# A written order for the last z units and the first gate pair of an encoder layer

## The chip, the core and the metric

The kernel runs on one core of a Trainium2 chip. A core has engines that run side by side, each with its own queue, taken in order: TensorE (PE; its weight loads are shown apart as PEld) multiplies matrices into banks of PSUM, VectorE (DVE) and ScalarE (ACT) work on elements, GpSimd (POOL) does a little of the rest, and SyncE (SP) issues transfers between the chip's memory and the on-chip buffers. The metric is device time in microseconds; lower is better. A run is repeated, and the median of the runs is the kernel's time. The profile comes from one execution of its own.

## The reference, cut to what matters

One layer: `h = RMSNorm(x)` with 16 meta tokens in front (1040 rows of 1024), one input projection `h @ w_in`, and its columns split into q, k, v, z, beta, a, three inputs of a short convolution, and two merge gates A and B of 1024 columns each. Then

```python
y_a = o_dn @ w_branch_dn[l]                      # gated DeltaNet over q, k, v, with silu(z)
y_b = (sc_b * depthwise_conv_centred(sc_c * sc_x, sc_conv_w[l])) @ w_branch_sc[l]
merged = jax.nn.sigmoid(gate_a) * y_a + jax.nn.sigmoid(gate_b) * y_b
h_res = h_res + merged @ w_out[l]
```

and a SwiGLU block and a last norm behind it. All is float32. The change concerns columns of `z`, of `gate_a` and of `gate_b`, and the start of `y_b`.

## The kernel before, in words

**Numbers in two parts.** Each float32 operand of a large product is split into a high and a low part (`split`, L100: ScalarE casts the high part, VectorE subtracts it from the source to get the low part). A product is three matmuls: high x high, high x low, low x high. So a weight of 128 columns (a *unit*, loaded by `wload`, L117) needs one transfer into a raw buffer, one cast on ScalarE (`wh`) and one subtraction on VectorE (`wl`) before its third matmul can run. `dense` (L129) runs the 8 x 3 matmuls of one unit with 512 rows of the activations.

**Phase 1** (to L1395) computes q, k and v, the DeltaNet scans, the short convolution, five of the eight z units (`ZH = 5`) and the gates of the first four column groups (`GH = 4`). It is written out by hand for every engine (`tc.manual_schedule()`, L1035). When its buffers are closed, the pool `tp` takes their place (L1399).

**The z section** (L1475 to L1487) computes the z units 5, 6 and 7. For each unit and each half of the rows: 24 matmuls into a bank (`psany` deals out the eight banks in turn), a tanh on ScalarE (L1485) and a finish on VectorE (L1486) that reads the bank; then a store to `z_d`. The weights have two buffers for `wh` and two for `wl`, so a third unit waits until the first one's matmuls are done. There are four raw buffers.

**The sums of blocks.** The gates 4 to 7 come in pairs, gate A and gate B of the same group, by a Strassen-like scheme with seven products of 512 x 512 blocks instead of eight. It needs sums of blocks of the activations, T1 to T4, which `moving_sums` (L1442) forms once: three or so VectorE operations of 128x2048 for each (`sub`, L179; `add`, L1409), then a split of each into a tile of its own (b0 to b3). Its work tiles are mA (t1, t2) and mB (t3 and a spare, d_). T2 is made from T1's sum, T4 from T2's.

**The pairs.** `pair` (L1492) loads the two weights rg and ru, splits rg whole (A11, A12) and the lower half of ru (A22), forms four sums of the weights' blocks in place (`sums`, L1414) and splits them into a tile `s_hl` (`stationary2`, L1421), which lies in mB for the pairs 0 and 2, in mA for 1 and 3. Then the products (`product`, L1434, 12 matmuls each, L1440) in the order A11 x B11, A12 x B21, S2 x T2, S1 x T1, S3 x T3, S4 x B22, A22 x T4; several of them add to a bank that ScalarE or VectorE has read in between. The last pair has an order of its own: S2, S3, S1, A22 x T4, A11, A12, S4.

**The branch.** Behind the pairs the short convolution's output p is loaded (L1570): its groups 0 to 3 into `mg[0]`, which lies in mA, 4 and 5 into two of four 128x1024 buffers (`s4`), 6 and 7 into raw buffers. It is split into b0 to b3, where T1 to T4 were (high parts in b0 and b1, low parts in b2 and b3). The first unit of `w_branch_sc` is multiplied with all eight groups, one after the other. The merge then writes `mg[0]` and `mg[1]` (mA and mB).

**Who sets the order.** Outside the hand-written stretches a planner orders each engine's queue when the program is built: by priority, earlier lines first, and by the times at which it reckons operands to be ready. Each queue then runs in that order, whatever the chip's times are. `tc.manual_schedule(engines=...)` holds the operations that are issued inside it, on the engines named, to the order in which they are written. Before the change the z section and the pairs are all left to the planner.

Of the kernel before, what the change touches and what calls it, by code (L numbers as in the profile page):

```python
# [8 lines left out]
F32 = mybir.dt.float32  # L9
# [7 lines left out]
P = 128  # L17
D = 1024
KT = 8
SEQ = 1024  # L20
META = 16
L = SEQ + META
C0 = 48
LP = C0 + L
H = 8
# [3 lines left out]
ZH = 5  # L29
GH = 4  # L30
# [7 lines left out]
def unit(col):  # L38

    return (col if col < OBA else col - 32) // P  # L40
# [8 lines left out]
def encoder_layer(ctx: ExitStack, tc: tile.TileContext, x, meta, norm1_w, w_in, w_ba,  # L49
# [3 lines left out]
    x, out = x[0], out[0]  # L53
# [15 lines left out]
    def s4(n=1024):  # L69
        return tp.tile([P, 1024], F32, tag="s4", name=uid("s4"), bufs=4)[:, :n]  # L70
# [29 lines left out]
    def split(hi, lo, src):  # L100
        nc.scalar.copy(hi, src)  # L101
        nc.vector.tensor_tensor(out=lo, in0=src, in1=hi.bitcast(F32), op=ALU.subtract)  # L102
# [14 lines left out]
    def wload(src, j):  # L117
        wh, wl, raw = staged([P, KT, P])
        nc.sync.dma_start(raw, src[j])
        split(wh, wl, raw)  # L120
        return wh, wl
# [7 lines left out]
    def dense(po, w, xx, t0, n, m=P):  # L129
        wh, wl = w  # L130
        xh, xl = xx
        for k in range(KT):
            xhk, xlk = (x[k] if isinstance(x, list) else x[:, k] for x in (xh, xl))
            mm(po[:m, :n], wh[:, k, :m], xhk[:, t0:t0 + n], start=(k == 0), stop=False)  # L134
            mm(po[:m, :n], wh[:, k, :m], xlk[:, t0:t0 + n], start=False, stop=False)  # L135
            mm(po[:m, :n], wl[:, k, :m], xhk[:, t0:t0 + n], start=False, stop=(k == KT - 1))  # L136
# [41 lines left out]
    def sub(out, a, b):  # L178
        nc.vector.tensor_tensor(out=out, in0=a, in1=b, op=ALU.subtract)  # L179
# [1221 lines left out]
    def big(tag, shape, dtype=F32R):  # L1401
        return tp.tile(shape, dtype, tag=tag, name=uid(tag))
# [9 lines left out]
    mov = {}  # L1412

    def sums(rg, ru, s2, s4_, s3, s1):  # L1414
        g0, g1, u0, u1 = rg[:, 0:4], rg[:, 4:8], ru[:, 0:4], ru[:, 4:8]
        nc.vector.tensor_tensor(out=s1, in0=u0, in1=u1, op=ALU.add)
        sub(s3, g0, u0)
        sub(s2, s1, g0)
        sub(s4_, g1, s2)

    def stationary2(j, ru, sa, sb, A_):  # L1421

        for i, r in enumerate((sa, sb)):
            sh, sl = (s_hl[j % 2][:, m, i] for m in range(2))
            split(sh, sl, r)
            for x, n in enumerate((("S2", "S4"), ("S3", "S1"))[i]):
                A_[n] = sh[:, 4 * x:4 * x + 4], sl[:, 4 * x:4 * x + 4]

# [13 lines left out]
    def moving_sums():  # L1442

        c = [slice(C0 + META + 512 * i, C0 + META + 512 * i + 512) for i in range(2)]
        f = lambda m: m.bitcast(F32)
        h0, h1 = ([f(hx[0][:, 4 * i:4 * i + 4, cc]) for cc in c] for i in range(2))
        l0, l1, l2 = ([f(t[:, :, cc]) for cc in c] for t in low_tiles)
        for i in range(2):
            for j in range(2):
                mov[f"B{i + 1}{j + 1}"] = hx[0][:, 4 * i:4 * i + 4, c[j]], [hx[1][4 * i + k][:, c[j]] for k in range(4)]  # L1450
        for i, n in enumerate(("T1", "T2", "T3", "T4")):
            t = big(f"b{i}", [P, 2, 4, 512])
            mov[n] = t[:, 0], t[:, 1]
        x, y = (big(g, [P, 2, 4, 512], F32) for g in ("mA", "mB"))
        t1, t2, t3, d_ = x[:, 0], x[:, 1], y[:, 0], y[:, 1]
        a, b = slice(0, 2), slice(2, 4)
        sub(t1, h0[1], h0[0])
        sub(d_, l0[1], l0[0])
        add(t1, t1, d_)
        split(*mov["T1"], t1)  # L1460
        sub(t2, h1[1], t1)
        add(t2[:, a], t2[:, a], l1[1])
        add(t2[:, b], t2[:, b], l2[1])
        split(*mov["T2"], t2)
        sub(t3, h1[1], h0[1])
        sub(d_[:, a], l1[1], l0[1][:, a])
        sub(d_[:, b], l2[1], l0[1][:, b])
        add(t3, t3, d_)
        split(*mov["T3"], t3)
        sub(t1, h1[0], t2)  # L1470
        add(t1[:, a], t1[:, a], l1[0])
        add(t1[:, b], t1[:, b], l2[0])
        split(*mov["T4"], t1)

    raw_slots.extend((tp, f"raw{i}") for i in range(2))  # L1475
    weights_z = [wload(w_in, unit(OZ + ZH * P))]
    moving_sums()
    for h in range(ZH, H):
        w = weights_z.pop() if weights_z else wload(w_in, unit(OZ + h * P))
        sz = s4(SEQ)  # L1480
        for i in range(2):
            po = psany()
            dense(po, w, hx, C0 + META + 512 * i, 512)
            sl = slice(512 * i, 512 * i + 512)
            nc.scalar.activation(sz[:, sl], po, AF.Tanh, scale=0.5)  # L1485
            nc.vector.scalar_tensor_tensor(out=sz[:, sl], in0=sz[:, sl], scalar=1.0, in1=po, op0=ALU.add, op1=ALU.mult)  # L1486
        nc.sync.dma_start(z_d[h], sz)  # L1487

    left, right = slice(0, 512), slice(512, 1024)
    half_turn = lambda o: nc.scalar.activation(o, o, AF.Tanh, scale=0.5)  # L1490

    def pair(n, j):  # L1492

        last = j == KT - 1
        s_hl[n % 2] = big(("mB", "mA")[n % 2], [P, 2, 2, KT, P])
        if n == 0:
            u = big("w2", [P, 2, 4, P])
            u_hl[0] = u[:, 0], u[:, 1]
        elif n == 1:
            u_hl[1] = [tp.tile([P, 4, P], F32R, tag="t2", name=uid("u_hl"), bufs=2) for _ in range(2)]  # L1500
        gh, gl = wtiles([P, KT, P])
        rg, ru = (rawtile([P, KT, P]) for _ in range(2))
        nc.sync.dma_start(rg, w_in[unit(OGA + j * P)])
        nc.sync.dma_start(ru, w_in[unit(OGB + j * P)])
        A_ = {"A11": (gh[:, 0:4], gl[:, 0:4]), "A12": (gh[:, 4:8], gl[:, 4:8])}
        o1, o2 = s4(), s4()
        bank = pss()
        if not last:
            split(gh, gl, rg)
            product(bank, A_["A11"], "B11")  # L1510
            nc.scalar.copy(o1[:, left], bank)
            po = psz()
            product(po, A_["A12"], "B21")
            add(o1[:, left], po, o1[:, left])
            half_turn(o1[:, left])
        split(*u_hl[n % 2], ru[:, 4:8])
        A_["A22"] = u_hl[n % 2]
        if last:
            split(gh, gl, rg)
        sums(rg, ru, rg[:, 0:4], rg[:, 4:8], ru[:, 0:4], ru[:, 4:8])  # L1520
        stationary2(n, ru, rg, ru, A_)
        bank2 = psz()
        if not last:
            product(bank, A_["S2"], "T2", True)
            nc.scalar.copy(o1[:, right], bank)
            product(bank2, A_["S1"], "T1")
            nc.scalar.copy(o2[:, right], bank2)
            product(bank, A_["S3"], "T3", True)
            add(o2[:, right], bank, o2[:, right])
            half_turn(o2[:, right])  # L1530
            product(bank2, A_["S4"], "B22", True)
            add(o1[:, right], bank2, o1[:, right])
            half_turn(o1[:, right])
            product(bank, A_["A22"], "T4", True)
            nc.scalar.activation(o2[:, left], bank, AF.Tanh, scale=0.5)
        else:
            product(bank, A_["S2"], "T2")
            nc.scalar.copy(o1[:, right], bank)
            product(bank, A_["S3"], "T3", True)
            nc.scalar.copy(o2[:, right], bank)  # L1540
            product(bank2, A_["S1"], "T1")
            add(o2[:, right], bank2, o2[:, right])
            product(bank, A_["A22"], "T4", True)
            po = psz()
            product(po, A_["A11"], "B11")
            nc.scalar.copy(o1[:, left], po)
            add(o2[:, left], bank, o1[:, left])
            half_turn(o2[:, left])
            add(o2[:, right], o2[:, right], o1[:, left])
            half_turn(o2[:, right])  # L1550
            add(o1[:, right], o1[:, right], o1[:, left])
            product(po, A_["A12"], "B21", True)
            nc.scalar.activation(o1[:, left], po, AF.Tanh, scale=0.5)
            product(bank2, A_["S4"], "B22", True)
            add(o1[:, right], bank2, o1[:, right])
            half_turn(o1[:, right])
        nc.sync.dma_start(ta_d[j], o1)
        nc.sync.dma_start(tb_d[j], o2)
        return o1

    for n, j in enumerate(range(GH, KT)):
        o1 = pair(n, j)

    warm2 = keep.tile([P, 1], F32, name="warm2")
    nc.scalar.activation(warm2, o1[:, SEQ - 1:SEQ], AF.Silu)
    mg = [big("mA", [P, 4, SEQ], F32), big("mB", [P, 4, SEQ], F32)]
    px = four("p")
    for j in range(KT):
        pr = mg[0][:, j] if j < 4 else s4(SEQ) if j < 6 else rawtile([P, SEQ])
        nc.sync.dma_start(pr, p_d[j])  # L1570
        split(px[0][j], px[1][j], pr)
    ox = (ap_.tile([P, KT, SEQ], F32R, tag="ah", name="oh"), eighths(low([SEQ])))
# [130 lines left out]
    t = KT - 1  # L1703
# [229 lines left out]
```

## Time and profile before

| what | us |
|---|---|
| median of 3 runs (2020.31 to 2021.19) | 2020.97 |
| the profiled execution | 2023.88 |
| its span, first to last instruction | 2022.2 |
| TensorE busy in the span | 1980.3 |
| VectorE busy | 1398.3 |
| ScalarE busy | 838.1 |
| mean granted clock of TensorE | 0.992 |

Times in the views count from the span's start; the z section begins at about 971 and the branch at about 1095. In a row of a timeline stand the start, the length, engine, line of the program, operation, the tile written and the tiles read, and the count of merged instructions; in brackets, the idle time before it and what ended it. A line is often that of a helper: L102 is the subtraction of any split, L101 its cast, L179 any `sub`, L1409 any `add`, and L134 to L136 the three matmuls of `dense`. Tiles are named without their numbers: `b` is any of b0 to b3, `s` any of the `s4` buffers, `pd`, `pe` and `pm` are banks. Matmuls overlap, so the length of one (0.39 us for 512 columns) is more than the step from one to the next.

### The profile page before, as it was taken

What the parts mean: (1) busy time and instruction counts of PE and PEld (TensorE: products, weight loads), DVE (VectorE), ACT (ScalarE), POOL (GpSimd) and SP (SyncE); (2) the same over time, 40 slices, a digit from 0 to 9 for tenths busy, and PEclk for the clock granted to TensorE, in tenths of its full rate; (3) what the DMA queues carried; (4) which work ended last, traced back from release to release, by engine and by line L of the source; (5) the groups of instructions that cost most, each with busy time, mean ns of one, the idle gap of its engine ahead of it and who ended that gap; (6) DMA issues with size and microseconds to landing.
All of it is one profiled execution on the core that took longest, in us unless ns stands there. A gap on an engine that the chain in (4) does not pass through costs nothing.

```text
span 2022.2 us, 31878 instructions
## 1 busy us (share of the span) xinstructions
PE 1980.3 (98%) x12011; PEld 1724.5 (85%) x12011; DVE 1398.3 (69%) x3013; ACT 838.1 (41%) x1961; POOL 109.2 (5%) x407
## 2 busy tenths in 40 slices
PE   9999999999999999999798999999999999999998
PEld 8998889899999999999687888887878888888887
DVE  6887678877888888855854544468856567656575
ACT  6463464536463646333244221224323333334344
POOL 2011101010201010100000000000000000000000
PEclk9999999999999999999899999999999999999999
DMA  3123231222221212121236643123665345477654
GB/s 136 62 88 100 74 94 59 95 58 85 64 69 59 74 58 74 58 74 53 83 115 243 223 147 116 58 89 106 237 219 209 136 165 175 159 270 245 195 175 166
DMA packets 131121, 251.00 MB, mean 124 GB/s; under 512 B 45013, under 2 KB 54662, under 8 KB 128535
## 3 DMA queue, kind: packets, MB, share of 16 engines
q1 hardware_dynamic: 130391, 247.92, 36.7%
q8 instruction: 94, 1.54, 0.3%
q10 hardware_dynamic: 576, 1.05, 0.1%
q14 instruction: 60, 0.49, 0.1%
HBM read 180.67 MB, written 68.25 MB: 123 GB/s over the span
## 4 chain that ended last, share of the span: by engine, by line
PE 88%; DVE 6%; DMA 3%; ACT 2%; issue 1%; SPq 0%; DVEq 0%; ACTq 0%
PE pm L341 32%; PE pd L1440 11%; PE pe L1440 5%; PE pm L1440 3%; PE pd L903 1%; PE pd L882 1%; PE pd L866 1%; PE pe L603 1%; PE pd L136 1%; PE pd L135 1%; PE pd L134 1%; PE pd L869 1%; PE pe L1839 1%; PE pe L1841 1%; PE pe L1840 1%; PE pd L899 1%
## 5 line engine op out<-in xcount | busy, mean ns | idle before, releaser
L341 PE MATMUL pm<-hTh,wh 128*128 128x512 f32 (+4 forms) x1296 | 446.9, 350 | 0.4 <-ACT hTh L1103 0.2
L341 PE MATMUL pm<-al,wh 128*128 128x512 f32 (+4 forms) x1296 | 446.2, 349 | 0.0
L341 PE MATMUL pm<-hTh,wl 128*128 128x512 f32 (+4 forms) x1296 | 444.1, 348 | 0.0
L341 PEld LDWEIGHTS pm<-hTh,wh 128*128 128x128 f32 x1296 | 242.9, 189 | 13.6 <-issue 0.8
L341 PEld LDWEIGHTS pm<-al,wh 128*128 128x128 f32 x1296 | 243.1, 189 | 12.4 <-issue 0.4
L341 PEld LDWEIGHTS pm<-hTh,wl 128*128 128x128 f32 x1296 | 243.1, 189 | 12.3 <-issue 0.4
L102 DVE TENSOR_TENSOR al<-raw,ring_h 128x1024 fp32r<-128x1024 f32 x73 | 88.8, 1223 | 65.3 <-ACT ring_h L101 64.5
L101 ACT CAST ring_h<-raw 128x1024 fp32r<-128x1024 f32 x73 | 76.6, 1053 | 108.5 <-PE pd L1841 33.7
L990 DVE TENSOR_TENSOR wl<-raw,wh 128x512 fp32r<-128x512 f32 x118 | 79.5, 688 | 30.6 <-ACT wh L993 30.2
L363 DVE SCALAR_TENSOR_TENSOR kq<-ra,wc,kq 128x520 f32<-128x520 f32 x128 | 96.8, 756 | 4.9 <-ACT kq L393 3.6
L889 ACT ACTIVATE w<-pd,small 128x128 f32<-128x128 f32 x128 | 40.0, 364 | 117.0 <-PE pd L882 116.5
L101 ACT CAST wh<-raw 128x1024 fp32r<-128x1024 f32 x47 | 49.4, 1051 | 91.5 <-PE pe L135 27.4
L496 DVE TENSOR_TENSOR tm<-fP,fN 128x135 f32<-128x135 f32 (+23 forms) x248 | 72.2, 291 | 4.9 <-DVE fP L500 0.2
L500 DVE TENSOR_TENSOR fP<-fP,tm 128x135 f32<-128x135 f32 (+23 forms) x248 | 71.7, 289 | 5.1
L993 ACT CAST wh<-raw 128x512 fp32r<-128x512 f32 x118 | 69.2, 621 | 3.7 <-issue 3.6
L102 DVE TENSOR_TENSOR wl<-raw,wh 128x1024 fp32r<-128x1024 f32 x47 | 57.4, 1220 | 8.1 <-ACT wh L101 8.0
L1409 DVE TENSOR_TENSOR b<-pd,b 128x512 f32<-128x512 f32 x22 | 15.2, 690 | 68.5 <-PE pd L1440 68.5
L1776 ACT ACTIVATE b<-b 128x512 f32<-128x512 f32 x22 | 13.9, 632 | 116.4 <-DVE b L1409 116.4
L856 ACT ACTIVATE jk<-NP 128x128 f32<-128x128 f32 x64 | 19.9, 310 | 83.6 <-DVE NP L852 82.6
L876 DVE SCALAR_TENSOR_TENSOR r<-pd,negEG,vS 128x128 f32<-128x128 f32 x120 | 36.8, 345 | 25.5 <-PE pd L866 24.9
L1440 PE MATMUL pd<-b_hl,wh 128*128 128x512 f32 x176 | 54.4, 390 | 0.0
L912 DVE SCALAR_TENSOR_TENSOR S<-S,eGl,pd 128x128 f32<-128x128 f32 x104 | 31.6, 342 | 30.4 <-PE pd L899 30.0
(588 smaller groups left out, 4696.1 us busy)
## 6 DMA issues: line engine op xcount, KB each, us to landing
raw<-in_w_in_dram SPq DMA_DIRECT2D x72, 512.0 KB
raw<-in_w_gate_up_dram SPq DMA_DIRECT2D x44, 512.0 KB
sums<-in_w_down_dram SPq DMA_DIRECT2D x22, 512.0 KB
t_d<-sums SPq DMA_DIRECT2D x11, 1024.0 KB
raw<-s_d SPq DMA_DIRECT2D x44, 256.0 KB
raw<-t_d SPq DMA_DIRECT2D x44, 256.0 KB
act_d<-b SPq DMA_DIRECT2D x43, 256.0 KB
raw<-act_d SPq DMA_DIRECT2D x33, 256.0 KB
```

What stands on the lines that cost most here:

```text
L101: nc.scalar.copy(hi, src)
L102: nc.vector.tensor_tensor(out=lo, in0=src, in1=hi.bitcast(F32), op=ALU.subtract)
L341: mm(po[:, :n], ww[:, k], f(k)[:, t0:t0 + n], start=i == 0, stop=i == 3 * KT - 1)
L363: nc.vector.scalar_tensor_tensor(out=acc, in0=raw[:, h0 + t:h0 + t + hn], scalar=wc[:, t, col:col + 1], in1=acc, op0=ALU.mult, op1=ALU.add)
L496: nc.vector.tensor_tensor(out=tv, in0=fP[:, 0:r, j:j + 1].broadcast_to([P, r, n]), in1=fN[:, j:j + 1, j + 1:32].broadcast_to([P, r, n]), o ...
L500: nc.vector.tensor_tensor(out=fP[:, 0:r, j + 1:32], in0=fP[:, 0:r, j + 1:32], in1=tv, op=ALU.subtract)
L876: nc.vector.scalar_tensor_tensor(out=r0[d], in0=b1[:, d], scalar=negEG[:, c, hd[d]:hd[d] + 1], in1=vS[:, c], op0=ALU.mult, op1=ALU.add)
L889: nc.scalar.activation(w[d], b2[:, 2 + d], AF.Copy, scale=ce[:, c, d:d + 1])
L912: nc.vector.scalar_tensor_tensor(out=Sn, in0=S[d], scalar=eGl[:, cd[d], hd[d]:hd[d] + 1], in1=b1[:, d], op0=ALU.mult, op1=ALU.add)
L990: nc.vector.tensor_tensor(out=u[1][1][:, k], in0=u[2][:, k], in1=u[1][0][:, k].bitcast(F32), op=ALU.subtract)
L993: nc.scalar.copy(u[1][0][:, k], u[2][:, k])
L1440: mm(po, x[:, k], y, start=k + i == 0 and not add_to, stop=k == 3 and i == 2, skip_group_check=add_to)
```

## The change

Three things are changed.

1. The z section and pair 0 stand inside a written order for VectorE and TensorE (`border0`), closed behind pair 0. ScalarE and SyncE are still ordered by the planner. Inside, the sums of blocks are cut into four steps (`moving_sums` becomes a generator), and so are the three z units (`z_rows`), with a step's end behind each tanh; the steps are dealt out by hand: T1, weights of unit 6, left half of unit 5, right half, T2, weights of unit 7, the last finish of unit 5, the loads of pair 0, left half of unit 6, first split of pair 0, right half of unit 6, the other splits and the sums of pair 0's weights, left half of unit 7, T3, right half of unit 7, T4, last finish, pair 0. A finish stands at the start of the step behind its tanh's.
2. `pair` is divided into `pair_weights` (buffers, loads, and two functions that issue the splits and sums) and the products. For the pairs 1 to 3 the order of issue stays as it was. The work tile of T3 and the spare move from mB to b3, and T4's tile is taken from b3 behind them; mB is first taken by pair 0's `s_hl`.
3. The groups 0 to 3 of p are loaded into `mg[1]` (mB) instead of `mg[0]` (mA), since `GH % 2 == 0` is 1. Where the merge writes stays as it was.

The diff:

```diff
@@ -1448,50 +1448,58 @@
         for i in range(2):
             for j in range(2):
                 mov[f"B{i + 1}{j + 1}"] = hx[0][:, 4 * i:4 * i + 4, c[j]], [hx[1][4 * i + k][:, c[j]] for k in range(4)]
-        for i, n in enumerate(("T1", "T2", "T3", "T4")):
+        for i, n in enumerate(("T1", "T2", "T3")):
             t = big(f"b{i}", [P, 2, 4, 512])
             mov[n] = t[:, 0], t[:, 1]
-        x, y = (big(g, [P, 2, 4, 512], F32) for g in ("mA", "mB"))
+        x, y = (big(g, [P, 2, 4, 512], F32) for g in ("mA", "b3"))
         t1, t2, t3, d_ = x[:, 0], x[:, 1], y[:, 0], y[:, 1]
         a, b = slice(0, 2), slice(2, 4)
         sub(t1, h0[1], h0[0])
         sub(d_, l0[1], l0[0])
         add(t1, t1, d_)
         split(*mov["T1"], t1)
+        yield
         sub(t2, h1[1], t1)
         add(t2[:, a], t2[:, a], l1[1])
         add(t2[:, b], t2[:, b], l2[1])
         split(*mov["T2"], t2)
+        yield
         sub(t3, h1[1], h0[1])
         sub(d_[:, a], l1[1], l0[1][:, a])
         sub(d_[:, b], l2[1], l0[1][:, b])
         add(t3, t3, d_)
         split(*mov["T3"], t3)
+        yield
+        t = big("b3", [P, 2, 4, 512])
+        mov["T4"] = t[:, 0], t[:, 1]
         sub(t1, h1[0], t2)
         add(t1[:, a], t1[:, a], l1[0])
         add(t1[:, b], t1[:, b], l2[0])
         split(*mov["T4"], t1)
+        yield
 
     raw_slots.extend((tp, f"raw{i}") for i in range(2))
-    weights_z = [wload(w_in, unit(OZ + ZH * P))]
-    moving_sums()
-    for h in range(ZH, H):
-        w = weights_z.pop() if weights_z else wload(w_in, unit(OZ + h * P))
+    left, right = slice(0, 512), slice(512, 1024)
+    border0 = ExitStack()
+    border0.enter_context(tc.manual_schedule(engines={mybir.EngineType.DVE, mybir.EngineType.PE}))
+    z_units = [wload(w_in, unit(OZ + ZH * P))]
+
+    def z_rows(h):
+
         sz = s4(SEQ)
-        for i in range(2):
+        for sl in (left, right):
             po = psany()
-            dense(po, w, hx, C0 + META + 512 * i, 512)
-            sl = slice(512 * i, 512 * i + 512)
+            dense(po, z_units[h - ZH], hx, C0 + META + sl.start, 512)
             nc.scalar.activation(sz[:, sl], po, AF.Tanh, scale=0.5)
+            yield
             nc.vector.scalar_tensor_tensor(out=sz[:, sl], in0=sz[:, sl], scalar=1.0, in1=po, op0=ALU.add, op1=ALU.mult)
         nc.sync.dma_start(z_d[h], sz)
-
-    left, right = slice(0, 512), slice(512, 1024)
+        yield
+
     half_turn = lambda o: nc.scalar.activation(o, o, AF.Tanh, scale=0.5)
 
-    def pair(n, j):
-
-        last = j == KT - 1
+    def pair_weights(n, j):
+
         s_hl[n % 2] = big(("mB", "mA")[n % 2], [P, 2, 2, KT, P])
         if n == 0:
             u = big("w2", [P, 2, 4, P])
@@ -1503,22 +1511,35 @@
         nc.sync.dma_start(rg, w_in[unit(OGA + j * P)])
         nc.sync.dma_start(ru, w_in[unit(OGB + j * P)])
         A_ = {"A11": (gh[:, 0:4], gl[:, 0:4]), "A12": (gh[:, 4:8], gl[:, 4:8])}
+
+        def first():
+            split(gh, gl, rg)
+
+        def second():
+            split(*u_hl[n % 2], ru[:, 4:8])
+            A_["A22"] = u_hl[n % 2]
+            sums(rg, ru, rg[:, 0:4], rg[:, 4:8], ru[:, 0:4], ru[:, 4:8])
+            stationary2(n, ru, rg, ru, A_)
+        return A_, first, second
+
+    def pair(n, j, A_, first, second):
+
+        last = j == KT - 1
         o1, o2 = s4(), s4()
         bank = pss()
         if not last:
-            split(gh, gl, rg)
+            if n:
+                first()
             product(bank, A_["A11"], "B11")
             nc.scalar.copy(o1[:, left], bank)
             po = psz()
             product(po, A_["A12"], "B21")
             add(o1[:, left], po, o1[:, left])
             half_turn(o1[:, left])
-        split(*u_hl[n % 2], ru[:, 4:8])
-        A_["A22"] = u_hl[n % 2]
         if last:
-            split(gh, gl, rg)
-        sums(rg, ru, rg[:, 0:4], rg[:, 4:8], ru[:, 0:4], ru[:, 4:8])
-        stationary2(n, ru, rg, ru, A_)
+            first()
+        if n:
+            second()
         bank2 = psz()
         if not last:
             product(bank, A_["S2"], "T2", True)
@@ -1558,15 +1579,37 @@
         nc.sync.dma_start(tb_d[j], o2)
         return o1
 
+    sums_of_blocks = moving_sums()
+    z0, z1, z2 = (z_rows(h) for h in range(ZH, H))
+    next(sums_of_blocks)
+    z_units.append(wload(w_in, unit(OZ + (ZH + 1) * P)))
+    next(z0)
+    next(z0)
+    next(sums_of_blocks)
+    z_units.append(wload(w_in, unit(OZ + (H - 1) * P)))
+    next(z0)
+    pair0 = pair_weights(0, GH)
+    next(z1)
+    pair0[1]()
+    next(z1)
+    pair0[2]()
+    next(z1)
+    next(z2)
+    next(sums_of_blocks)
+    next(z2)
+    next(sums_of_blocks)
+    next(z2)
     for n, j in enumerate(range(GH, KT)):
-        o1 = pair(n, j)
+        o1 = pair(n, j, *(pair_weights(n, j) if n else pair0))
+        if n == 0:
+            border0.close()
 
     warm2 = keep.tile([P, 1], F32, name="warm2")
     nc.scalar.activation(warm2, o1[:, SEQ - 1:SEQ], AF.Silu)
     mg = [big("mA", [P, 4, SEQ], F32), big("mB", [P, 4, SEQ], F32)]
     px = four("p")
     for j in range(KT):
-        pr = mg[0][:, j] if j < 4 else s4(SEQ) if j < 6 else rawtile([P, SEQ])
+        pr = mg[GH % 2 == 0][:, j] if j < 4 else s4(SEQ) if j < 6 else rawtile([P, SEQ])
         nc.sync.dma_start(pr, p_d[j])
         split(px[0][j], px[1][j], pr)
     ox = (ap_.tile([P, KT, SEQ], F32R, tag="ah", name="oh"), eighths(low([SEQ])))
```

## The prediction

> **What bounds the kernel now.** I read the page first, then the list of waits of TensorE, then the stretches around the two long waits, then the chain and the timelines of the engines there.
>
> ```profile
> PE 1980.3 (98%) x12011; PEld 1724.5 (85%) x12011; DVE 1398.3 (69%) x3013; ACT 838.1 (41%) x1961; POOL 109.2 (5%) x407
> PE pd L136 <- DVE wl L102: 11.5, 1, 11.5
> PE pd L134 <- ACT b L101: 6.0, 1, 6.0
> 992.90:1006.40 13.50, 1.97 (x8) 0.99 (x6) 13.50 (x11) 5.07 (x4) 0.00 (x0) 0.70 0.12 47
> 1006.40:1012.20 5.80, 5.79 (x14) 4.59 (x15) 5.73 (x6) 0.99 (x2) 0.00 (x0) 0.52 0.49 163
> 1094.70:1100.70 6.00, 0.01 (x1) 0.00 (x0) 3.34 (x4) 4.09 (x5) 0.00 (x0) 0.72 0.99 358
> 1100.70:1104.20 3.50, 3.44 (x7) 2.32 (x8) 2.10 (x2) 1.50 (x2) 0.00 (x0) 0.51 1.01 410
> ```
>
> TensorE is busy 98% of the span, so only its waits can be won. The two longest stand at the two ends of the stretch that the change touches; the columns of a stretch are length, busy time of PE, PEld, DVE, ACT and POOL, then the granted clock. Each wait is followed by a stretch at half clock: 5.8 us at 0.52 and 3.5 us at 0.51, a further loss of 5.8 x 0.48 = 2.8 us and 3.5 x 0.49 = 1.7 us.
>
> Why the first wait? The timeline of VectorE (first column the start, second the length):
>
> ```profile
> 961.04 1.23 DVE L102 TENSOR_TENSOR wl<-raw,wh 128x1024 fp32r<-128x1024 f32 x1
> 962.18 1.53 DVE L416 SCALAR_TENSOR_TENSOR rb<-ra,cols,rb 128x512 f32<-128x512 f32 x2
> 971.05 0.69 DVE L451 TENSOR_TENSOR rb<-pm,rb 128x512 f32<-128x512 f32 x1 [4.70 <-PE pm L341]
> 971.91 1.23 DVE L102 TENSOR_TENSOR wl<-raw,wh 128x1024 fp32r<-128x1024 f32 x1 [0.17 <-ACT wh L101]
> 973.91 2.29 DVE L179 TENSOR_TENSOR mA<-hTh 128x2048 f32<-128x2048 f32 x1 [0.77 <-DMA p_d<-rb]
> 976.12 2.28 DVE L179 TENSOR_TENSOR mB<-al 128x2048 f32<-128x2048 f32 x1
> 980.52 2.29 DVE L1409 TENSOR_TENSOR mA<-mA,mB 128x2048 f32<-128x2048 f32 x1
> 982.72 0.68 DVE L1486 SCALAR_TENSOR_TENSOR s<-s,pm 128x512 f32<-128x512 f32 x1
> 987.72 2.35 DVE L1409 TENSOR_TENSOR mA<-mA,al 128x1024 f32<-128x1024 f32 x2
> 1005.14 1.22 DVE L102 TENSOR_TENSOR wl<-raw,wh 128x1024 fp32r<-128x1024 f32 x1
> 1010.33 0.69 DVE L1416 TENSOR_TENSOR raw<-raw 128x512 f32<-128x512 f32 x1
> 1011.66 0.68 DVE L102 TENSOR_TENSOR u_hl<-raw,u_hl 128x512 fp32r<-128x512 f32 x1
> ```
>
> The low parts of units 5 and 6 were cut at 961.04 and 971.91, that of unit 7 only at 1005.14, behind 31 us of sums for T1 to T4. TensorE had nothing else that was ready. The section's account, from TensorE's rows:
>
> ```profile
> 1026.52 2.72 PE pe L1440 x12
> 1034.51 2.88 PE L1440 MATMUL pd<-b,w 128*128 128x512 f32 x12
> 1053.55 2.88 PE L1440 MATMUL pd<-b,u_hl 128*128 128x512 f32 x12
> ```
>
> Twelve matmuls take 2.72 us, 0.227 each. From 971.05 (phase 1's last product is done there, its reader L451 starts) three z units of 48 are 32.6 us and two gate pairs of 84 are 38.1, together 70.7. The other two rows are the last products, A22 x T4, of pairs 0 and 1. Pair 1 so ends at 1053.55 + 2.72 = 1056.3, so 85.2 us were spent: **14.5 us** are the wait and its slow clock.
>
> **The change, part by part.**
>
> *1. The first half of the section.* No operation goes and none comes; the order changes. A full-width sum starts 2.2 us after the one before it (973.91, 976.12), two half-width ones are 2.27, a cut of one weight 1.14 to the next start, a z finish (L1486) 0.60, each of the four 512-wide sums 0.69. Written order adds what the planner had avoided: behind each T-block's sums stands its cut, which waits for ScalarE's cast:
>
> ```profile
> 983.19 1.90 ACT L101 CAST b<-mA 128x2048 fp32r<-128x2048 f32 x1
> 1011.83 1.05 ACT L101 CAST mB<-raw 128x1024 fp32r<-128x1024 f32 x1 [1.05 <-DVE raw L179]
> ```
>
> With 0.1 us on either side that is a hole of 2.1 us on VectorE for each T-block and 1.15 for a weight. The sums cannot start before 973.91, because the first is released by the last store of phase 1 and that does not move. Then:
>
> - T1: 3 x 2.2 + 2.1 + 2.2 = 10.9, to 984.8; unit 6's low part to 986.0. Before, it was done at 973.1. TensorE needs it at 971.05 + 10.88 + 0.45 = 982.4, so there is a **new wait of 3.7 us**, queued behind T1 on VectorE. Should unit 5's cut now also stand behind phase 1's last operation (971.74), 1.4 us of the 3.7 fall at unit 5; the sum is the same.
> - T2: 2.2 + 2.27 + 2.1 + 2.2 = 8.8; with two z finishes and unit 7's low part, VectorE is at 997.0 and unit 7's part is ready at 996.5. TensorE ends unit 6 at 986.05 + 46 x 0.227 = 996.5: **no wait for unit 7**, the 11.5 us are gone.
> - Pair 0's first cut needs unit 6's buffers, free at 996.5, and a cast: 998.9. Finish, 22-block, four sums, a hole of 1.15, two cuts, finish: 1006.9. TensorE comes to pair 0 at 1007.4, so its weights cost nothing; unit 7's matmuls cover them.
> - T3 is 11.0, to 1017.9; a finish and T4 8.8, to 1027.2; then a finish and two of pair 0's additions, the second of which must have read the bank that A22 x T4 adds to: **1029.1**.
>
> TensorE, from 1007.4, runs A11, A12, S2, S1 to 1018.3 (T3 is in time), S3 and S4 to 1023.7. Then the last product would wait 5.4 us for T4: that is late next.
>
> Whether TensorE stands still there depends on the planner. It holds only operations inside the written order to that order, and before's trace shows it slipping others in: the cut at 961.04 belongs to unit 5, but stands between two operations of phase 1, which is in written order. The second such border, behind the merge, shows the same:
>
> ```profile
> 1397.01 0.69 DVE L102 TENSOR_TENSOR u_hl<-raw,u_hl 128x512 fp32r<-128x512 f32 x1
> 1400.41 0.68 DVE L1416 TENSOR_TENSOR raw<-raw 128x512 f32<-128x512 f32 x1
> 1401.86 2.29 DVE L102 TENSOR_TENSOR b<-al,b 128x2048 fp32r<-128x2048 f32 x1
> 1403.01 0.73 PE L1440 MATMUL pe<-s,s_hl 128*128 128x512 f32 x2 [0.62 <-ACT s_hl L101]
> 1404.20 4.38 PE L1440 MATMUL pd<-b,w 128*128 128x512 f32 x11 [0.47 <-DVE b L102]
> ```
>
> There the weight sums of the next pair (1397.01, 1400.41) stand ahead of the written T4 cut at 1401.86, and a piece of the next pair's product ran while A22 x T4 waited. TensorE was not in written order there, so for it this is an inference from VectorE. I take it that pair 1's A11 and A12, 5.4 us, fill the gap. Pair 1's cuts and sums (1.1 + 0.6 + 2.8 = 4.5 us) then slip into VectorE's holes for T3 and T4 (2 x 2.1); what doesn't fit delays the written chain, between 0.3 us and all 4.5, and I take 1.5, since the holes are nearly as long as the work. That makes about 0.6 us of wait at S3, 0.8 at A22 and 0.5 at pair 1's S2.
>
> Sum: 3.7 + 0.6 + 0.8 + 0.5 = 5.6 us of waits instead of 14.5: **8.9 us won** by the end of pair 1. The pairs behind it leave VectorE room to catch up (third and fourth number: 19 us of TensorE, 8.95 of VectorE):
>
> ```profile
> 1037.30:1056.30 19.00, 19.00 (x86) 15.73 (x85) 8.95 (x11) 7.69 (x12) 0.00 (x0) 1.00 0.31 111
> 962.30 0.34 SPq L1504 DMA_DIRECT2D raw<-in_w_in_dram  x1
> ```
>
> The queue of SyncE: pair 0's second load left at 962.30 already (second row), into the raw buffer that unit 5 gives up, and the written order doesn't hold SyncE. The three z stores leave with the right-hand finishes, near 997, 1007 and 1028 by the sums above; pair 1 needs the last of their buffers for o2 only after its S1 product, some 12 us later. I cost them at nothing.
>
> *2. The branch operands.*
>
> ```profile
> 1072.75 5.44 PE pd L1440 x24
> 1083.76 2.72 PE pd L1440 x12
> 1086.48 8.24 PE pe L1440 x36
> 1094.74 4.86 DMA mA<-p_d
> 1099.62 1.05 ACT b L101
> 1083.86 0.69 DVE L1409 TENSOR_TENSOR s<-pe,s 128x512 f32<-128x512 f32 x1 [10.37 <-PE pe L1440]
> 1086.58 1.23 DVE L102 TENSOR_TENSOR b<-s,b 128x1024 fp32r<-128x1024 f32 x1 [2.03 <-PE pd L1440]
> 1093.79 1.23 DVE L102 TENSOR_TENSOR wl<-raw,wh 128x1024 fp32r<-128x1024 f32 x1 [0.78 <-ACT wh L101]
> ```
>
> mA holds the last pair's weights, read until 1094.7; only then does the load start, and load, cast and semaphores are the 6.0 us. mB holds pair 2's, whose last reader ends at 1072.75. The four loads (4 of 512 KB, 5.8 us at the 358 GB/s of the stretch above) can be in by about 1082. Their cuts go where T1 and T3 lay, free at 1083.76. What is late next is those cuts: four casts, 4 us, and four subtractions, 4.6 us, beside the last three products, 8.2 us. VectorE stood idle 10.4 us before 1083.86 and 2.03 + 0.78 = 2.8 us from there to 1094.7, so some of the later additions move past the end, but the branch's first matmuls need only the first operands, one each 0.45 us or more. I cost this at nothing; if the cover were short, it would be up to 2 us. **Won: 6.0 + 1.7 = 7.7 us.**
>
> Moving T3's work tile from mB to b3 costs nothing by itself: T4 takes b3 after T3's cut in the same order.
>
> Together 16.6 us. The profiled execution took 2023.88 us with a span of 2022.2, 2.9 above the median of 2020.97; differences carry over, so **2020.97 - 16.6 = 2004.4**.
>
> *A rule weighed.* After the broken-up waits at 1401.8 the clock fell as well:
>
> ```profile
> 1404.20:1408.60 4.40, 4.39 (x12) 3.50 (x13) 2.89 (x4) 0.85 (x2) 0.00 (x0) 0.61 0.75 253
> ```
>
> That was 2.60 + 0.62 + 0.47 = 3.7 us of waiting, 4.4 x 0.39 = 1.7 us lost. The Trainium skill (TensorE: Matmul & The Clock Gate, Part 1: The HAM clock gate) says the clock halves after an idle window of about 3.4 us, whose phase is free, and comes back after as much work. By that rule the new 3.7 us wait just reaches the point, and would cost an estimated 1.7 us; the trace agrees with it at 3.7, 6.0 and 11.5 us.
>
> **The rivals.**
>
> - *Nothing fills the T4 gap* (TensorE's written order lets nothing by). Against it: the rows of 961.04 and 1397.01; for it: TensorE itself isn't shown. Waits 3.7 + 5.4, and 1.7 of slow clock as after the 6.0 us wait: 10.8, won 3.7 + 7.7 = 11.4, **2009.6**.
> - *The clock falls at unit 6.* For it: the row at 1404.20; against it: unit 5's share may cut the wait in two. 16.6 - 1.7: **2006.1**.
> - *The branch loads don't arrive earlier* (they queue behind stores, or the cuts are late): change 2 does nothing, 8.9 alone, **2012.1**.
> - *Slower: ScalarE's order.* ScalarE isn't in written order. If the planner puts the T casts behind z's tanhs, each cast waits for half a unit of matmuls, up to 5.4 us, and VectorE, strictly in order, waits with it: up to 4 x 5.4 = 21.8 us on the chain, **2031** without filling. It turns the sign once more than 11.4 us, over two casts, are lost. Against it: the T1 cast of before (983.19) started 0.4 us behind its sum (980.52 + 2.29), though z finishes went on around it. One or two casts held gives about 2018 to 2021.
>
> **How the numbers follow.** Forecast 0.50, no filling 0.22, clock 0.10, branch loads 0.08, ScalarE's order 0.10 (0.06 slower, 0.04 within the bound). A measurement of this kernel tells about 0.2%, 4 us. Faster 0.90, same 0.04, slower 0.06. The forecast's own range is 2001.5 to 2008 (up to 3 us of delay on the written chain, or all holes filled with T3 in time); with the rivals down to the branch loads, 2001.5 to 2012.5.
>
> **What would show it.** No TensorE wait for unit 7's wl; one of 3 to 4 us for unit 6's (or 1.4 and 2.3); pair 0's A22 x T4 starting near 1029 to 1031 (before: 1034.5), with pair 1's A11 and A12 ahead of it if filled; loads of p into mB at about 1070 and no wait of the first branch matmul. The forecast is wrong if unit 6's wait is over 6 us, if the T casts start over 1 us behind their sums, or if the branch still waits for b.

## The result, and the profile after

The changed kernel takes **2003.59 us**, the median of five runs (2001.8 to 2004.27), against 2021.19 for the kernel before beside it; the ratio is 0.9909, with a 95% interval of 0.9895 to 0.9922. The kernel was run twice more with later experiments: 2005.3 against 2021.22 (0.9919, 0.9906 to 0.9933) and 2005.12 against 2020.05 (0.9923, 0.9910 to 0.9937; one of those five runs took 8821 us and is left out of the ratio). The forecast was 2004.4.

The two kernels differ in order up to the branch only. So besides the whole time I read one stretch of each profile: from the start of phase 1's last operation on VectorE to the first matmul of the first product behind the projection. These are rows of VectorE's and TensorE's timelines, first of the kernel before (its other end, 971.05, is shown in the prediction), then of the changed kernel.

```profile
1370.00 0.71 PE L1440 MATMUL pd<-b_hl,wh 128*128 128x512 f32 x2
```

```profile
970.38 0.69 DVE L451 TENSOR_TENSOR rb<-pm,rb 128x512 f32<-128x512 f32 x1 [4.70 <-PE pm L341]
1353.44 0.71 PE L1440 MATMUL pd<-b_hl,wh 128*128 128x512 f32 x2
```

The stretch shrinks from 398.95 to 383.06 us. In the two further profiles of the changed kernel it is 383.42 and 382.38, so **16.0 us** are won in it by the mean of the three (382.95), and a difference under 1 us between single profiles says nothing. The kernel before has one profile only. The three differences of the medians, 17.6, 15.9 and 14.9 us, lie around that; what the parts behind the stretch add or take varies from run to run.

The busy times on the changed kernel's page, the same work in a shorter span:

```profile
PE 1977.3 (99%) x12011; PEld 1724.1 (86%) x12011; DVE 1396.6 (70%) x3013; ACT 836.4 (42%) x1961; POOL 107.8 (5%) x407
```

And the head of its list of TensorE's waits (matmul, what ended the wait; total, times, longest):

```profile
PE pe L136 <- DVE wl L102: 3.8, 1, 3.8
PE pd L1440 <- ACT b L101: 2.6, 1, 2.6
```

The 11.5 us for a unit's low part and the 6.0 us ahead of the branch are gone. One wait of 3.8 us has come; the next row, 2.6 us, is an old one of the feed-forward. In the stretches of the section (length; busy time of PE, PEld, DVE, ACT, POOL; granted clock) TensorE stands still in the first and runs slowly in the second, and is busy through all the others:

```profile
970.40:985.50 15.10, 11.28 (x50) 9.01 (x48) 10.93 (x7) 5.36 (x6) 0.00 (x0) 0.94 0.26 88
985.50:990.80 5.30, 5.29 (x13) 4.19 (x14) 5.11 (x4) 0.12 (x1) 0.00 (x0) 0.52 0.29 99
990.80:1007.30 16.50, 16.50 (x75) 13.64 (x74) 10.76 (x13) 7.04 (x8) 0.00 (x0) 1.00 0.21 64
1007.30:1034.50 27.20, 27.20 (x120) 22.17 (x119) 25.00 (x21) 11.04 (x13) 0.00 (x0) 1.00 0.21 71
```

VectorE's timeline shows why, and where T3 and T4 now stand:

```profile
982.03 2.29 DVE L102 TENSOR_TENSOR b<-mA,b 128x2048 fp32r<-128x2048 f32 x1 [1.98 <-ACT b L101]
984.24 1.22 DVE L102 TENSOR_TENSOR wl<-raw,wh 128x1024 fp32r<-128x1024 f32 x1
994.83 1.22 DVE L102 TENSOR_TENSOR wl<-raw,wh 128x1024 fp32r<-128x1024 f32 x1
999.55 1.23 DVE L102 TENSOR_TENSOR wl<-raw,wh 128x1024 fp32r<-128x1024 f32 x1 [2.90 <-ACT wh L101]
1014.78 1.22 DVE L102 TENSOR_TENSOR wl<-raw,wh 128x1024 fp32r<-128x1024 f32 x1
1018.72 1.22 DVE L102 TENSOR_TENSOR wl<-raw,wh 128x1024 fp32r<-128x1024 f32 x1
1020.46 2.28 DVE L102 TENSOR_TENSOR b<-b,b 128x2048 fp32r<-128x2048 f32 x1
1029.97 2.29 DVE L102 TENSOR_TENSOR b<-mA,b 128x2048 fp32r<-128x2048 f32 x1 [2.03 <-ACT b L101]
```

The first row is T1's cut, behind the 1.98 us hole for its cast, and unit 6's low part stands behind it. Unit 7's follows at 994.83, pair 0's at 999.55. The cuts at 1014.78 and 1018.72 are those of pairs 1 and 2, slipped in ahead of T3's cut (1020.46); T4's is at 1029.97. On TensorE, A22 x T4 then starts at

```profile
1034.52 2.91 PE L1440 MATMUL pd<-b,w 128*128 128x512 f32 x12
1047.69 2.88 PE L1440 MATMUL pd<-b,u_hl 128*128 128x512 f32 x12
1086.08 0.39 PE L134 MATMUL pd<-b,wh 128*128 128x512 f32 x1
```

which is where it started before (1034.51). But pair 1's own last product, the second row, starts 5.9 us earlier than the 1053.55 of before, since its first products were done while pair 0 waited for T4. Counted from phase 1's last operation, which starts 0.67 us earlier here, that is 5.2 us, and 12 matmuls of pair 2 (2.7 us) were done ahead of it too: 7.9 us. The third row is the branch's first matmul, with no wait ahead of it.

### The profile page after: what moved, and what is told of

The parts are those of the page before. It is cut to its first block, busy times and chain, and to the rows that moved or that the text cites. A ratio compares the mean times of both kernels' runs of the same rounds, so it can differ in the third digit from the quotient of the medians.

```text
span 2002.5 us, 31873 instructions
## 1 busy us (share of the span) xinstructions
PE 1977.3 (99%) x12011; PEld 1724.1 (86%) x12011; DVE 1396.6 (70%) x3013; ACT 836.4 (42%) x1961; POOL 107.8 (5%) x407
## 4 chain that ended last, share of the span: by engine, by line
PE 90%; DVE 4%; DMA 3%; ACT 1%; issue 1%; SPq 0%; DVEq 0%; ACTq 0%
PE pm L341 33%; PE pd L1440 12%; PE pe L1440 5%; PE pm L1440 3%; PE pd L903 1%; PE pd L882 1%; PE pd L866 1%; PE pe L136 1%; PE pe L134 1%; PE pd L869 1%; PE pe L135 1%; PE pe L603 1%; PE pd L134 1%; PE pd L136 1%; PE pd L135 1%; PE pe L1882 1%
```

## The experiments

Each kernel is the changed one with one edit, unless the edit says otherwise. "Stretch" is the one defined above.

| kernel | median us (lowest to highest) | ratio to before (95%) | stretch us |
|---|---|---|---|
| before, beside the others | 2021.19, 2021.23, 2021.22, 2020.05 | 1 | 398.95 |
| changed, three times | 2003.59, 2005.3, 2005.12 | 0.9909, 0.9919, 0.9923 | 383.06, 383.42, 382.38 |
| branch operands alone | 2011.58 (2010.81 to 2012.16) | 0.9950 (0.9938 to 0.9963) | 390.30 |
| written order alone | 2012.01 (2011.38 to 2013.46) | 0.9953 (0.9941 to 0.9966) | 390.98 |
| TensorE written through all pairs | 2014.97 (2013.67 to 2018.11) | 0.9969 (0.9957 to 0.9982) | 394.43 |
| third and fourth pair held | 2005.2 (2004.71 to 2007.14) | 0.9927 (0.9913 to 0.9940) | 384.91 |
| written order for VectorE alone | 2002.44 (2001.89 to 2004.42) | 0.9909 (0.9896 to 0.9923) | 381.28 |
| idle transposes in the wait | 2003.19 (2002.14 to 2003.7) | 0.9911 (0.9897 to 0.9924) | 383.35 |
| unit 6 cut ahead of T1 | 2000.58 (1999.04 to 2003.35) | 0.9898 (0.9884 to 0.9911) | 379.59 |
| units 6 and 7 cut early, twice | 1997.26, 1997.21 | 0.9882, 0.9885 (0.9868 to 0.9898) | 376.56, 376.51 |

**1. The two parts, one at a time.** The theory: each part takes away a wait of its own, and they add up. First the branch operands alone, in the kernel before:

```diff
-        pr = mg[0][:, j] if j < 4 else ...
+        pr = mg[1][:, j] if j < 4 else ...
```

> The kernel before, with one edit: the groups 0 to 3 of p are loaded into mB instead of mA. My account: the wait of 6.0 us at the branch and the 1.7 us of slow clock behind it go, everything ahead of it stays, so 7.7 us less than before (about 2013.5), and no TensorE wait for b at the first branch matmul. Rival, that the place of the loads doesn't matter because the cuts into b0 to b3 are late anyway: same as before (2021), with the wait still there.

The time, 2011.58, is 2 us below what was expected; the stretch loses 8.65 us. In its list of waits, up to the branch, the 11.5 us are left, alone:

```profile
PE pd L136 <- DVE wl L102: 11.5, 1, 11.5
```

Then the written order alone, with p in mA as before:

```diff
-        pr = mg[GH % 2 == 0][:, j] if j < 4 else ...
+        pr = mg[0][:, j] if j < 4 else ...
```

> The kernel after, with the groups 0 to 3 of p loaded into mA as before. My account: what the z section wins (14.5 us less the wait of 3.8 and the 2.6 of slow clock at unit 6, so 8.1) stays, the branch's 7.7 go: about 2011.3. Rival, that the two parts overlap (the time won in front is lost again at the branch, or the branch's gain needs the front's): 2004 or 2021.

```profile
PE pd L134 <- ACT b L101: 6.2, 1, 6.2
PE pe L136 <- DVE wl L102: 3.8, 1, 3.8
```

The time is 2012.01, 0.7 us above what was expected, and the stretch loses 7.97 us. 8.65 + 7.97 = 16.6, against 16.0 for both together: within the spread of a profile, the parts add up.

**2. Does other work fill the wait for T4?** The forecast rested on the planner putting pair 1's products ahead of A22 x T4. Here all TensorE work of the four pairs is held to written order, so nothing can; VectorE's order is that of the changed kernel.

```diff
     border0 = ExitStack()
+    border_pe = ExitStack()
+    border_pe.enter_context(tc.manual_schedule(engines={mybir.EngineType.PE}))
     border0.enter_context(tc.manual_schedule(engines={mybir.EngineType.DVE, mybir.EngineType.PE}))
...
             border0.close()
 
+    border_pe.close()
```

> The kernel after, with TensorE held to written order through all four pairs; VectorE's order stays as it is. So TensorE can't run pair 1's and pair 2's first products while pair 0 waits for T3 and T4. My account: it waits about 2.4 us for T3 and 5.9 for T4, with 1.7 to 2.6 us of slow clock behind the second: 10 to 11 us more than the kernel after, about 2014. Rival, that the filling is worth nothing, because the pairs behind wait for VectorE instead: about 2004.

Beside unit 6's 3.8 us its list of waits has:

```profile
PE pd L1440 <- DVE s L1409: 5.9, 1, 5.9
PE pd L1440 <- DVE b L102: 2.1, 1, 2.1
```

And its stretches, the first the wait of A22 x T4, the second behind it:

```profile
1028.40:1034.30 5.90, 0.02 (x1) 0.03 (x1) 4.23 (x5) 3.54 (x4) 0.00 (x0) 0.79 0.09 37
1034.30:1040.00 5.70, 5.70 (x16) 4.54 (x17) 2.95 (x4) 2.54 (x6) 0.00 (x0) 0.62 0.70 252
```

S3 waits 2.1 us for T3, A22 x T4 5.9 us for T4 and the addition that must have read the bank, and the clock falls once more (0.62 behind it); up to the branch only 0.7 us of other waits come. The time is 2014.97, where about 2014 was expected. The stretch is 11.5 us longer than the changed kernel's, and 4.1 longer than with the branch operands alone: **without the filling, the written order is a loss**. The filling is the gain of part 1.

**3. Whose products fill it?** By the order of TensorE's queue, 24 matmuls of pair 1 (A11, A12), 12 of pair 2 and 2 of pair 1's S2 stand between pair 0's products and its A22 x T4 in the changed kernel: 38 x 0.227 = 8.6 us. The forecast had counted on pair 1's alone. Here pairs 2 and 3 are held to written order among themselves, behind an unheld pair 1; 4 matmuls of pair 2 are left ahead.

```diff
         if n == 0:
             border0.close()
+        if n == 1:
+            border_pe = ExitStack()
+            border_pe.enter_context(tc.manual_schedule(engines={mybir.EngineType.PE}))
+    border_pe.close()
```

> The changed kernel with TensorE's products of the third and fourth gate pair held to written order among themselves by a second border, so that fewer of the third pair's first products can slip ahead of pair 0's A22 x T4; pair 1's may still. In the changed kernel some 14 matmuls of the third pair (3 us) stand there. If they were what covered the 1.9 us that the forecast left over for S3, A22 and S2, waits of 2 to 3 us appear there and the time is 2 to 3 us above the changed kernel's: 2006 to 2007. Rival: pair 1's 24 matmuls are enough, and the third pair's only came early: 2003.5 to 2004.5, no new wait.

Beside unit 6's 3.8 us its list of waits has:

```profile
PE pd L1440 <- DVE s L1495: 1.4, 1, 1.4
PE pd L1440 <- ACT s L1559: 0.7, 1, 0.7
```

A wait of 1.4 us appears ahead of A22 x T4. The stretch is 2.0 us longer than the mean of the changed kernel and 2.5 longer than that of the same set of runs, whose profile lost as much clock at unit 6; the medians, 2005.2 and 2005.12, don't show it. 2005.2 lies between the two expectations. The stretch is for the theory that pair 2's matmuls covered what pair 1's left open, the whole time doesn't decide.

**4. Is it VectorE's order or TensorE's?** The border names both engines. The rival: TensorE's is needed too. Here it names VectorE alone.

```diff
-    border0.enter_context(tc.manual_schedule(engines={mybir.EngineType.DVE, mybir.EngineType.PE}))
+    border0.enter_context(tc.manual_schedule(engines={mybir.EngineType.DVE}))
```

> The changed kernel with the written order for VectorE alone; TensorE's order is the planner's. If the gain comes from the order of VectorE, this gives the changed kernel's time or, since the planner may put ready matmuls of later z units ahead of unit 6's low part, up to 2 us less: 2001.6 to 2003.6. Rival: TensorE's written order is needed, and the planner's own puts it behind T3 or T4 again: 2006 to 2012.

2002.44 against 2005.3 beside it. TensorE's written order isn't needed. The planner moves ready matmuls of later units into the wait for unit 6. TensorE's timeline, two rows of it:

```profile
984.55 0.50 PE L134 MATMUL pd<-hTh,wh 128*128 128x512 f32 x1 [1.34 <-ACT wh L101]
...
986.59 0.50 PE L136 MATMUL pe<-hTh,wl 128*128 128x512 f32 x1 [0.82 <-DVE wl L102]
```

The stretches, the first with both waits in it:

```profile
982.80:987.00 4.20, 2.03 (x8) 1.04 (x7) 3.89 (x3) 1.70 (x3) 0.00 (x0) 1.00 0.00 0
987.00:992.30 5.30, 5.30 (x25) 4.38 (x24) 4.69 (x4) 0.40 (x1) 0.00 (x0) 1.00 0.33 99
```

The wait falls in two, 1.34 and 0.82 us with four matmuls between them, and the clock stays at 1.00. The stretch is only 2.1 us shorter than that of the changed kernel beside it, since up to the branch its list of waits has two new ones, 1.0 and 0.5 us, for casts.

**5. Is the slow clock behind unit 6's wait a cost of its own?** 32 idle transposes, which `idle_turns` issues on the identity matrix, are put into the wait; VectorE's order, and so the start of unit 6's low part, stays.

```diff
     next(z0)
     next(z0)
+    idle_turns(32)
     next(sums_of_blocks)
```

> 32 idle transposes on TensorE (0.109 us each, 3.5 us) in written order between unit 5's last matmul and unit 6's first fill the wait for unit 6's low part; VectorE's order is untouched, so unit 6 starts no earlier. If the clock's fall behind that wait is a cost of its own (5.3 us at 0.52 loses 2.5 us), the clock stays at 1.00 behind the transposes and the time is 2.5 us lower than the changed kernel's: 2001.1. Rival: the slow stretch costs nothing at the end, because what follows (T4 on VectorE) sets the time anyway, or the clock falls all the same: 2003.6 to 2004.

```profile
981.33 3.65 PE L98 MATMUL pd<-ident 128*128 128x128 f32 x32
...
1032.91 2.89 PE L1440 MATMUL pd<-b,w 128*128 128x512 f32 x12
```

```profile
985.50:991.00 5.50, 5.23 (x23) 4.33 (x24) 5.38 (x5) 0.00 (x0) 0.00 (x0) 1.00 0.29 95
```

The first fence has two rows of TensorE's timeline, the second the stretch behind the wait. The clock stays at 1.00 (behind the wait it was 0.50 in the changed kernel beside it), and A22 x T4 starts at 1032.91 instead of 1035.12 in the changed kernel beside it, with phase 1's last operation at 970.64 in both: **2.2 us won there**. They don't last. In the next pair a wait of 1.5 us stands before an S4, which had not been there; ScalarE's timeline has its cause:

```profile
1042.46 1.05 ACT L101 CAST wh<-raw 128x1024 fp32r<-128x1024 f32 x1 [2.83 <-DMA raw<-in_w_in_dram]
1043.42 1.04 ACT L101 CAST mB<-raw 128x1024 fp32r<-128x1024 f32 x1
1044.36 0.58 ACT L1553 COPY s<-pm 128x512 f32<-128x512 f32 x1
```

The cast of a later pair's weight waits 2.83 us for its load, and the copy that frees the bank for S4 is queued behind it. Everything ran 2.2 us earlier, that load too (issued at 1034.89 instead of 1037.03), but its data came no sooner than at 1042.46, while in the changed kernel the cast started at 1041.74. Why this load took 7.6 us stays open. The stretch is the same as the changed kernel's (383.35 against 383.42). The median, 2003.19, is not the 2001.1 that was expected, and the 2.1 us between it and 2005.3 lie within the intervals. So the clock's fall cost 2.2 us where it fell, and in this kernel the wait behind a late load took 1.5 of them back. By the branch's first matmul 0.1 us is left (1086.60 against 1086.71); the other 0.6 us no single wait shows.

**6. Can the wait for unit 6 go altogether?** First unit 6's load and cut ahead of T1's sums.

```diff
+    z_units.append(wload(w_in, unit(OZ + (ZH + 1) * P)))
     next(sums_of_blocks)
-    z_units.append(wload(w_in, unit(OZ + (ZH + 1) * P)))
```

> The kernel after, with unit 6's weight cut ahead of T1's sums in VectorE's written order instead of behind them; VectorE is idle for 2.2 us at that place. My account: TensorE's wait of 3.8 us for unit 6 and the 2.6 us of slow clock behind it go; VectorE's chain ends about 4 us earlier, TensorE's 6.4, so up to 2.4 us may come back as a wait for T3 or T4: 1997 to 1999.6. Rival, that VectorE's chain to T4 bounds the section and the wait for unit 6 was slack: 2003.6, with the wait moved to S3 or A22 x T4.

```profile
994.64 0.50 PE L136 MATMUL pd<-hTh,wl 128*128 128x512 f32 x1 [2.42 <-DVE wl L102]
```

```profile
994.70:1000.00 5.30, 5.30 (x24) 4.38 (x25) 4.41 (x7) 0.87 (x2) 0.00 (x0) 1.00 0.67 198
```

The row of TensorE's timeline and the stretch behind it show why the time, 2000.58, is above what was expected: the wait isn't gone but has moved to unit 7, whose cut stands behind T2's, and is 2.42 us long. The clock does not fall behind it. The stretch is 3.4 us shorter than the changed kernel's mean. Expected were 1997 to 1999.6, so this missed by 1 us. Then unit 7's as well, ahead of T2's sums:

```diff
     next(z0)
     next(z0)
-    next(sums_of_blocks)
     z_units.append(wload(w_in, unit(OZ + (H - 1) * P)))
+    next(sums_of_blocks)
```

> Unit 6's load and cut ahead of T1's sums, and unit 7's ahead of T2's sums instead of behind its cut. If the 2.4 us wait that was left with unit 6 first comes only from unit 7's cut standing behind T2's, no TensorE wait is left in the section and the time is 2.4 us lower than that kernel's 2000.6: 1998.2, 5.4 below the changed kernel. Rival: the sums of T2 to T4, each 1.2 us later, are what is late next (S3 or A22 x T4 waits): 2000 to 2002.

> The version with both unit cuts moved forward once more: 1997.3 within 1.5, no wait of TensorE between phase 1's last matmul and the branch.

Its stretches, from unit 5 to A22 x T4 and from there to the branch:

```profile
970.20:1034.00 63.80, 63.80 (x282) 52.47 (x282) 56.85 (x50) 26.77 (x31) 0.00 (x0) 1.00 0.27 93
1034.00:1079.60 45.60, 45.60 (x201) 37.24 (x200) 25.75 (x30) 25.64 (x34) 0.00 (x0) 1.00 0.64 230
```

TensorE is busy without a gap and at full clock from phase 1 to the branch. 1997.26 and 1997.21 us: 0.9 less than was first expected. The stretch is 3.05 us shorter than with unit 6 alone, of which the wait is 2.42; the other 0.6 is less than single profiles differ by. This version beats both kernels, the changed one by 6.4 us in the stretch (382.95 - 376.54). By the rows of the changed kernel's three profiles, 3.8 us of waiting and 1.7 to 2.65 us of slow clock, 5.5 to 6.5 were to be won.

The changed kernel once more, beside experiments 4 and 5 and the first run of the last version, and beside experiment 3 and its second (the times are in the table):

> The changed kernel once more, as the base for the other three kernels on this chip: 2003.6 us within 1.5, the 3.8 us wait of TensorE for unit 6's low part, and a granted clock near 0.52 in the 5.3 us behind it.

> The changed kernel a third time, as the base for these: 2003.6 to 2005.3.

The first repeat, 2005.3, missed 2003.6 within 1.5 by 0.2 us; its wait was 3.8 us and the clock behind it 0.50, as expected. The second is within its range.

## Why the prediction was right, point by point

**Unit 6's wait.** Forecast 3.7 us, measured 3.83:

```profile
985.51 0.79 PE L136 MATMUL pe<-hTh,wl 128*128 128x512 f32 x1 [3.83 <-DVE wl L102]
```

The chain behind it held step by step: T1's first sum at 973.24, its cut at 982.03, the low part at 984.24. Unit 5's cut still slipped into phase 1, so the wait was not divided.

**The clock behind it: the term that was left out.** The sum took no loss of clock; it stood among the rivals at 1.7 us with 0.10. It happened in every profile with this wait, and its size varies: over the 5.3 us behind the wait the granted clock was 0.52, 0.50 and 0.50 in three of them (2.5 to 2.65 us lost: the changed kernel's first two and experiment 2's), and 0.68 in three others (1.7 us: the changed kernel's third, the order alone and experiment 3's). Most of the 1 us between the changed kernel's three stretches is this. These are 12 us around the wait in its first and in its third profile:

```profile
981.00:993.00 12.00, 8.17 (x25) 6.21 (x25) 8.96 (x7) 4.33 (x4) 0.00 (x0) 0.72 0.13 44
981.00:993.00 12.00, 8.17 (x29) 6.50 (x29) 9.55 (x7) 4.23 (x5) 0.00 (x0) 0.86 0.14 44
```

While it is down the clock is at 0.50 in both, read in steps of 0.5 us. So it was down for 12 x 0.28 x 2 = 6.7 us in the first and 3.4 us in the third. In the first it fell inside the wait (0.78 over 981.70 to 985.50), in the third only with the first matmuls behind it (1.00 over 981.10 to 984.90). The row of 0.61 behind 3.7 us of broken-up waiting, in the prediction, had said that the clock can fall here. The Trainium skill (TensorE: Matmul & The Clock Gate, Part 1: The HAM clock gate) has a window of about 3.4 us that runs free of the kernel; a cost that differs from profile to profile behind the same 3.83 us agrees with that, and so does the clock that stays up behind 2.42 us. What does not agree is that in the first profile the clock fell about 2.1 us into the wait (3.8 x 0.22 x 2 = 1.7 us before its end), ahead of a whole idle window; why it fell in six profiles of six stays open.

**No wait for unit 7, and pair 0's weights at nothing:** both right; TensorE is busy for all of 990.80 to 1034.50.

**T3 and T4 were mis-sized.** T3's cut ends at 1020.46 + 2.28 = 1022.7 and T4's at 1032.3, forecast 1017.9 and 1027.2: 5 us late; counted from phase 1's last operation (970.38 here, 971.05 in the forecast) 5.5 and 5.7 us. Counted so, pair 0's first cut, which ended at 1000.8 instead of 998.9, is 2.5 us late, which is the slow clock's loss (it needs unit 6's buffers); and the slipped work was larger: pair 1's cuts and sums, which were counted, and pair 2's cut at 1018.72, which was not. The hole for T3's cast swallowed 2 us of it. I had allowed 1.5. So A22 x T4 started at 1034.5, not at 1029 to 1031.

**The waits at S3, A22 and S2 were mis-sized the other way.** Forecast 1.9 us together, measured none, though T4 was later: not 24 but 38 matmuls were moved ahead (experiment 3). The inference that TensorE, too, lets other work past a written order was right, and it carries the gain: experiment 2 lost 11.5 us without it. The rival of no filling was priced too mildly at 2009.6, for it took T4 as on time.

Part 1 by the rows of the changed kernel's first profile: 3.8 us of waiting and 2.5 of clock, 6.3 instead of 5.6; 14.5 - 6.3 = 8.2 won. The order alone lost 1.7 us of clock at unit 6, so 9.0 by its rows, and 7.97 in its stretch: the account is good to about 1 us. That the sum held is in part luck, for three errors of up to 5 us nearly cancel: what is late on VectorE was hidden by what is early on TensorE.

**ScalarE's order**, the rival on the other side, did not come: each T cast follows its sum within 0.1 us. T1's sum ends at 980.05, the cast starts at

```profile
980.09 1.91 ACT L101 CAST b<-mA 128x2048 fp32r<-128x2048 f32 x1 [3.67 <-DVE mA L1409]
```

**The branch.** SyncE issues the loads into mB, first column the start, at

```profile
1064.32 0.33 SPq L1613 DMA_DIRECT2D mB<-p_d  x1
1068.04 1.87 SPq L1613 DMA_DIRECT2D mB<-p_d  x3
```

Forecast about 1070. ScalarE and VectorE had the first parts ready before pair 3 ended, and the first matmul followed it at full clock:

```profile
1066.80:1086.30 19.50, 19.50 (x86) 15.81 (x86) 10.59 (x12) 12.71 (x16) 0.00 (x0) 1.00 0.79 290
```

Forecast 7.7 us; the branch operands alone gave 8.65, and 8.0 on top of the written order (390.98 - 382.95), or 8.6 against the changed kernel's third profile (382.38), which like the order alone lost 1.7 us of clock at unit 6.

**The sum.** 16.6 forecast, 16.0 in the stretch, 14.9 to 17.6 by the medians. The clock came on top of the sum, the 1.9 us of later waits did not come, and the branch gave about 1 us more than its 7.7.

## What to carry to other kernels

A wait on TensorE that is caused by VectorE's order can be shortened without a faster VectorE, by asking which result TensorE needs first; one cut of 1.2 us, moved ahead of 11 us of sums and their cut, was worth 3.4 us here, and a second one 3 more. A written order on one engine pays if the other engines may still run other work past it: look in the queue for what is ready, count its matmuls against the gap, and hold as few engines as you can. And where a wait nears the length behind which the trace shows the clock fall (3.7 us here, not 2.4), price the clock as well.

## What was not expected of the hardware

The same wait of 3.83 us, at the same place, cost 1.7 us of clock in some profiles and 2.6 in others, and in the two that are shown the clock was down for 3.4 and 6.7 us; a wait of 2.42 us and one of 1.34 + 0.82 cost none, and 32 idle transposes (3.65 us) in the wait kept the clock at 1.00. A load of 512 KB, issued 2.1 us earlier, was landed no earlier: 7.6 us from issue to the cast that waited for it, against 4.7 us at most.
